# A layer trunk on one core: seven-product block multiplications in the feed-forwards, from four groups of k tiles to five, and their products redistributed over the stage

## The chip, the cores and the metric

One Trainium2 chip, one of its cores. The metric is the device time of one execution in microseconds (us); of several runs of a kernel the median is taken. A TensorE instruction works on tiles of 128 partitions; its results go to PSUM, whose banks hold 128x512 float32 each, and the kernel uses all eight of them. VectorE (DVE in the profile), ScalarE (ACT), GpSimd (POOL) and SyncE (SP) run beside TensorE (PE, and PEld for its weight loads), each in the order of its own instruction stream.

## What is computed

Two layers. Each is a half-step SwiGLU feed-forward, a token mixer, and a second half-step feed-forward, on 256 tokens of width 1024, so that four feed-forwards are run in all:

```python
def swiglu(x, w_in, w_out):
    gate, up = jnp.split(x @ w_in, 2, axis=-1)
    return (jax.nn.silu(gate) * up) @ w_out
...
for l in range(DEPTH):
    h = h + 0.5 * swiglu(rms_norm(h, ffn1_norm[l]), ffn1_w_in[l], ffn1_w_out[l])
    u = rms_norm(h, mix_norm[l])
    ...
    h = h + merged @ w_out[l]
    h = h + 0.5 * swiglu(rms_norm(h, ffn2_norm[l]), ffn2_w_in[l], ffn2_w_out[l])
return rms_norm(h, final_norm)
```

`w_in` is 1024 x 5632 and `w_out` 2816 x 1024, all float32. The change is about the second product of each feed-forward, (silu(gate) * up) @ w_out, whose contraction of 2816 is cut into 22 k tiles of 128. The mixer (a Mamba-2 branch and a gated DeltaNet branch) is not touched.

## The kernel before

**Precision by splitting.** Every float32 operand is split into a high part (rounded on ACT) and a low part (the rest, a subtraction on DVE). A product is three matmuls: high by high, high by low, low by high (`mm3` for token-stationary products at L335 to L337, `mm3w` for weight-stationary ones at L340 to L346). A weight tile of 128x1024 that has been split is called a form here: `prep` (L169 on) issues its ACT copy `whi` (L68) and its DVE subtraction `wlo` (L71).

**The weight stream.** `plan` lists the forms of the whole program in the order in which they are used, `stream` the loads. The loads go out on SP's queue into five buffers `wraw` (NRAW), the forms into five buffers each of `whi` and `wlo` (NSPL). `take` hands out the next form and on each call emits the preparation of forms up to four past it. After `state["hold"]` is set, it emits none beyond the form that it hands out. The tile framework allots a buffer of a pool when one is free, puts each engine's instructions in an order of its own making, by order of emission and by readiness in its model of time, and adds the waits.

**A feed-forward.** `ffn` runs the string `FFN`: `f` is the first 256 hidden columns with tokens stationary (four forms); each `c` is a chunk of 256 hidden channels' gate and up, 48 weight-stationary matmuls of 256 columns into one PSUM bank `fc` of the pool `accp` (four banks), with two forms. After a chunk ACT makes the SiLU (`sg`), DVE the product (`g`), and after every second chunk a pair of k tiles is split into the stationary operands `gh` and `gl`. Letters `A`, `B` and `d` are the second product, with tokens stationary, 128x512 at a time: token block t (two), column half n (two), k tile.

**Seven products for eight.** For the pairs of k tiles in `PAIRS` the 2x2x2 block product (two token blocks, two k tiles, two column halves) is done with seven products in the manner of Strassen and Winograd. Two pairs make a group. Each of a group's seven products is six 128x512 matmuls (two pairs by three) with one form; it would be eight directly. `block_sums` makes, per pair, four sums of 128x128 blocks on DVE and splits them (two ACT, two DVE instructions). The forms `q0` to `q2` have sums of weight tiles, each with one more DVE addition of 128x1024 in place; `q3` has a last addition done by an accumulating DMA on POOL's queue (`add_to`, L156), whose sum `q6` uses. The summed tile `wsum` stands in one of four buffers y0 to y3 from the first stage until its `q6`.

Before, the string is `f`, eight `c`, `A`, four `c`, `A`, four `c`, `A`, two `c`, `A`, two `c`, then `BdBBBddddd`. An `A` is four products of a group (into the four banks `p1`, `p5`, `p7`, `p6` of the pool `trp`), a `B` its other three, in the output banks `po` after the last chunk; two of a `B`'s forms are loaded a second time. Four groups cover 16 k tiles. The other six, `DIRECT`, are done directly by `d` (12 matmuls each).

**The end of a feed-forward.** `close_blocks` runs the `B`s and `d`s. `join` combines the four `p` banks into updates of the residual h, which go out as four accumulating DMAs on POOL's queue (L460). The last five `d` are taken at once and run token block 0 first: 30 matmuls, then 30 for token block 1. `residual` adds the `po` banks to h on DVE (`h<-o,h`); `norm_in` then makes the RMS norm of block 0, its eight PE transposes `hnT` being tied behind the sixth group of three matmuls of block 1 (`state["sums"][5]`), so that block 1's matmuls run during the norm. In the last feed-forward block 1's second column half is cut in two of 256 columns, the last of them in a bank `tail`.

Of the kernel before, what the change touches and what calls it, by code (L numbers as in the profile page):

```python
# [49 lines left out]
def trunk_kernel(ctx, tc, x, wst, wsm, norms, lpar, rpar, cst, out):  # L54
# [52 lines left out]
    def plan_ffn(j):  # L107


        o, j2, held = j + 4 * FC, j + 4 * FC + 22, []  # L110
# [63 lines left out]
    def prep(i):  # L174
        kind, js, _ = plan[i]
        hi = wpool.tile([P, 1024], F32R, tag="whi", name="whi", bufs=NSPL)
        lo = wpool.tile([P, 1024], F32R, tag="wlo", name="wlo", bufs=NSPL)
        r = raws[js[0]]
        with ExitStack() as behind:
            for ins in state["behind"].pop(i, ()):  # L180
                behind.enter_context(tc.issue_after(ins))
            state["whi"] = act(hi[:], r[:])
            if kind in ("q1", "q2"):
                to, by = (raws[k][:] for k in js[1:])
                tt(to, to, by, ALU.add)
# [7 lines left out]
        for k in {"q0": (), "q1": (), "q2": js[::2], "q3": ()}.get(kind, (js[0],)):  # L193
            raws.pop(k)
        halves[i] = (hi, lo)

# [247 lines left out]

    def block_products(todo, begin, end):

        for bank, st, prs in todo:
            wh, wl = take()
            for i, p in enumerate(prs):
                sh, sl = st(p)  # L450
                c = slice(i * 512, (i + 1) * 512)
                mm3(bank[:], sh, sl, wh[:, c], wl[:, c], begin and i == 0, end and i == 1)
# [21 lines left out]
    def close_blocks(po, stat, sums, pb, nw):  # L474

        direct, joined, n = list(DIRECT), join(pb), 0
        rest = FFN[FFN.rindex("c") + 1 :]
        for kind in rest[: len(rest) - NSPL]:  # L480
            if kind == "d":
                k = direct.pop(0)
                out_chunks(po, stat, [k], None, first=k == DIRECT[0])
                continue
            todo = [
                (po[0][1], lambda p: sums(p, 3), PAIRS[n]),
                (po[0][0], lambda p: stat(2 * p + 1, 0), PAIRS[n]),
                (po[1][0], lambda p: stat(2 * p + 1, 1), PAIRS[n]),
            ]
            block_products(todo, n == 0, False)  # L490
            n += 1
            if n % 2 == 0:
                next(joined)
        state["hold"] = True
        if nw is None:
            po.append(trb("tail"))
        out_chunks(po, stat, direct, direct[-1], group=NSPL, split=nw is None, first=False)
        return residual(po, nw)


    def ffn(nxt):
        gh = [slots.tile([P, 8, S], F32R, tag=t_, name="gh") for t_ in ("sA", "sB", "sC")]
# [1 line left out]

        bsa = slots.tile([P, 2, 2, 3, P], F32R, tag="sG", name="bsa")
        bsb = slots.tile([P, 16, P], F32R, tag="sH", name="bsb")
        bsc = slots.tile([P, 4, 2, P], F32R, tag="sI", name="bsc")
        bsd = s2.tile([P, 2, 2, P], F32R, tag="s2", name="bsd")
        bsb3 = bsb[:, 0:12].rearrange("p (i o j) t -> p i o j t", i=2, o=2)
        bsb1 = bsb[:, 12:16].rearrange("p (i o) t -> p i o t", i=2)  # L510

        def sums(p, j):

            q, i = (p - 1) // 2, (p - 1) % 2
# [3 lines left out]
            b = (bsc[:, 0:2], bsc[:, 2:4], bsb1, bsd[:])[q]  # L518
            return b[:, i, 0, :], b[:, i, 1, :]

        def block_sums(p, g2):

            sf = tmp2("sf")
            a11, a21, a12, a22 = (g2[:, j * P : (j + 1) * P] for j in range(4))
            s1, s2_, s3, s4 = (sf[:, j * P : (j + 1) * P] for j in range(4))
            tt(s1, a21, a22, ALU.subtract)
            tt(s3, a11, a21, ALU.subtract)
            tt(s2_, s1, a11, ALU.subtract)
            tt(s4, a12, s2_, ALU.add)
            q, i = (p - 1) // 2, (p - 1) % 2  # L530
# [20 lines left out]
        for t in range(2):  # L551
# [2 lines left out]
            tt(sg[:, 256:512], sg[:, 0:256], ps[t][:, 256:512], ALU.mult)  # L554
            gt.append(sg[:, 256:512])
        todo, pb, n, cut = FFN[1:], {}, 0, False
        for c in range(FC - 1):
            g2 = tmp2("g2")
            for a in range(2):
# [13 lines left out]
            split(2 * c + 2, g2[:].rearrange("p (k t) -> p k t", k=2))  # L573
            if c + 1 <= PAIRS[-1][-1]:
                block_sums(c + 1, g2)
            if todo[0] == "A":
                if not pb:
                    pb.update({i: trb(f"p{i}") for i in (1, 6, 5, 7)})
                four = [
                    (pb[1], lambda p: stat(2 * p, 0), PAIRS[n]),  # L580
                    (pb[5], lambda p: sums(p, 0), PAIRS[n]),
                    (pb[7], lambda p: sums(p, 2), PAIRS[n]),
                    (pb[6], lambda p: sums(p, 1), PAIRS[n]),
                ]
                block_products(four, n == 0, n == len(PAIRS) - 1)
                todo, cut = todo[1:], True
                n += 1
        po = [[accb("o"), accb("o")] for _ in range(2)]

        return close_blocks(po, stat, sums, pb, nxt)  # L590


    def mixer(l, nxt):
# [714 lines left out]
def _layout(inp):  # L1308
# [20 lines left out]
    def blocks(w):  # L1329
# [109 lines left out]
```

## Time and profile before

| | |
|---|---|
| time of three runs | 1543.58, 1544.32, 1544.55 us, median 1544.32 |
| span of the profiled execution, first to last instruction | 1539.7 us |
| PE, DVE, ACT, POOL busy | 99%, 80%, 61%, 5% of the span |
| mean rate of all DMA | 199 GB/s |
| feed-forwards in the trace (start to start of the next stage) | 591.7 to 769.2 us, 769.2 to 946.7 us, for instance |

The runs are 4.6 us longer than the profiled span at the median: what lies before the first and after the last instruction of the trace, and differences between executions. No other time of the profiled execution is given. A busy time counts from an instruction's start to its modelled end, and matmuls overlap one another, so that the step from one start to the next is what a matmul costs, not its duration; the same holds, by less, on DVE.

### The profile page before, as it was taken

To read this page: it belongs to the slowest core of one execution; us is meant where nothing else is said; L and a number is where in the kernel's file an instruction comes from. 1 tells how busy PE (TensorE), PEld (TensorE's weight loads), DVE (VectorE), ACT (ScalarE), POOL (GpSimd) and SP (SyncE) were. 2 spreads that over 40 slices of the span, in tenths; PEclk is the share of its full clock that TensorE was granted. 3 is DMA by queue.
4 is the path that set the end of the run, shared out by engine and by line. 5 is a ranking of instruction groups with operands and counts; after the bars stand their busy time and mean duration, and the time that the engine had idled before them with its cause. 6 is when DMAs were issued, how large, how long until landed. Compare 5 with 4: busy or idle time off the path is not lost.

```text
span 1539.7 us, 29072 instructions
## 1 busy us (share of the span) xinstructions
PE 1522.8 (99%) x11473; PEld 1384.4 (90%) x11473; DVE 1229.7 (80%) x1859; ACT 944.8 (61%) x1532; POOL 81.8 (5%) x92
## 2 busy tenths in 40 slices
PE   8999999999999999999999999999999999999998
PEld 7999889999888888999899998899998888899997
DVE  6878769967899766789778887689589996677886
ACT  5655667765665645555555566676756666455565
POOL 0000110000000000000100012010000000000010
PEclk9999999999999999999999999999999999999999
DMA  7687775653565556587867687665345555556785
GB/s 277 190 265 231 226 228 167 187 164 111 178 213 171 163 166 196 185 256 211 261 225 225 208 253 229 197 193 180 117 141 202 179 170 186 176 177 195 247 241 156
DMA packets 98831, 305.73 MB, mean 199 GB/s; under 512 B 22837, under 2 KB 23813, under 8 KB 97670
## 3 DMA queue, kind: packets, MB, share of 16 engines
q1 hardware_dynamic: 93796, 290.95, 57.2%
q0 software_dynamic: 4608, 12.58, 5.1%
q8 instruction: 90, 1.47, 0.4%
q14 instruction: 47, 0.39, 0.1%
q10 hardware_dynamic: 290, 0.33, 0.1%
HBM read 297.72 MB, written 1.92 MB: 195 GB/s over the span
## 4 chain that ended last, share of the span: by engine, by line
PE 89%; DVE 4%; ACT 2%; DMA 2%; issue 1%; SPq 1%; POOL 0%; POOLq 0%; ACTq 0%; DVEq 0%
PE fc L346 10%; PE fc L340 9%; PE fc L345 9%; PE t L366 9%; PE o L337 4%; PE o L335 4%; PE o L336 4%; PE f L366 3%; PE b L335 3%; PE b L337 3%; PE b L336 3%; PE p L336 2%; PE p L337 2%; PE p L335 2%; PE xs L345 1%; PE xs L340 1%
## 5 line engine op out<-in xcount | busy, mean ns | idle before, releaser
L71 DVE TENSOR_TENSOR wlo<-wraw,whi 128x1024 fp32r<-128x1024 f32 x488 | 591.8, 1221 | 186.7 <-ACT whi L68 172.2
L68 ACT ACTIVATE whi<-wraw 128x1024 fp32r<-128x1024 f32 x488 | 511.6, 1059 | 271.0 <-PE fc L345 92.5
L346 PE MATMUL fc<-uW,wlo 128*128 128x256 f32 x1280 | 354.9, 277 | 0.0
L340 PE MATMUL fc<-uW,whi 128*128 128x256 f32 x1280 | 354.1, 277 | 0.0
L345 PE MATMUL fc<-uW,whi 128*128 128x256 f32 x1260 | 348.3, 276 | 0.0
L340 PEld LDWEIGHTS fc<-uW,whi 128*128 128x128 f32 x1280 | 240.5, 188 | 0.8
L346 PEld LDWEIGHTS fc<-uW,wlo 128*128 128x128 f32 x1280 | 240.5, 188 | 0.0
L345 PEld LDWEIGHTS fc<-uW,whi 128*128 128x128 f32 x1260 | 236.5, 188 | 0.8
L366 PE MATMUL t<-whi,uW 128*128 128x512 f32 x512 | 165.3, 397 | 0.0
L366 PEld LDWEIGHTS t<-whi,uW 128*128 128x128 f32 x512 | 95.9, 188 | 21.6 <-issue 1.3
L68 ACT ACTIVATE whi<-wsum 128x1024 fp32r<-128x1024 f32 x64 | 68.0, 1062 | 58.8 <-PE fc L345 32.9
L366 PE MATMUL t<-wlo,uW 128*128 128x512 f32 x256 | 100.2, 392 | 0.0
L71 DVE TENSOR_TENSOR wlo<-wsum,whi 128x1024 fp32r<-128x1024 f32 x64 | 78.2, 1221 | 7.9 <-ACT whi L68 5.6
L335 PE MATMUL b<-whi,bh 128*128 128x512 f32 x192 | 76.1, 398 | 0.3
L336 PE MATMUL b<-wlo,bh 128*128 128x512 f32 x192 | 74.9, 390 | 0.0
L337 PE MATMUL b<-whi,bl 128*128 128x512 f32 x192 | 74.2, 393 | 0.0
L340 PE MATMUL xs<-uW,whi 128*128 128x256 f32 x256 | 72.8, 284 | 0.0
L346 PE MATMUL xs<-uW,wlo 128*128 128x256 f32 x256 | 71.4, 279 | 0.0
L345 PE MATMUL xs<-uW,whi 128*128 128x256 f32 x254 | 70.6, 278 | 0.0
L335 PE MATMUL o<-whi,gh 128*128 128x512 f32 (+1 forms) x160 | 62.0, 388 | 0.0
L337 PE MATMUL o<-whi,gl 128*128 128x512 f32 (+1 forms) x160 | 61.8, 386 | 0.0
L336 PE MATMUL o<-wlo,gh 128*128 128x512 f32 (+1 forms) x160 | 61.7, 386 | 0.0
(337 smaller groups left out, 3291.7 us busy)
## 6 DMA issues: line engine op xcount, KB each, us to landing
wraw<-in_wst_dram SPq DMA_DIRECT2D x504, 512.0 KB, 4.9
wsum<-in_wst_dram SPq DMA_DIRECT2D x16, 512.0 KB, 7.3
wsum<-in_wst_dram POOLq DMA_DIRECT2D x16, 512.0 KB, 8.7
dc<-rdram SPq DMA_DIRECT2D x8, 1024.0 KB, 8.5
nw<-in_norms_dram SPq DMA_DIRECT2D x6, 512.0 KB, 5.9
h<-u POOLq DMA_DIRECT2D x12, 256.0 KB, 6.8
gb<-rdram SPq DMA_DIRECT2D x8, 256.0 KB, 5.6
h<-in_x_dram SPq DMA_DIRECT2D x4, 256.0 KB, 3.7
```

The lines of the kernel that those rows point to most:

```text
L68: return A.activation(out=o, in_=i, func=func, **kw)
L71: return V.tensor_tensor(out=o, in0=a, in1=b, op=op)
L335: PE.matmul(ps, lh, rh, start=start, stop=False)
L336: PE.matmul(ps, lh, rl, start=False, stop=False)
L337: return PE.matmul(ps, ll, rh, start=False, stop=stop)
L340: PE.matmul(ps, wh, mh, start=start, stop=False)
L345: PE.matmul(ps, wh, ml, start=False, stop=False)
L346: PE.matmul(ps, wl, mh, start=False, stop=stop)
L366: ins = PE.matmul(ps[t][:], st, mv, start=k0 == 0 and j == 0, stop=k0 == KT - 2 and j == 5)
```

## The change

Five groups cover 20 of the 22 k tiles (`PAIRS` from (0, 1) to (8, 9)); two, 20 and 21, stay direct. An `A` is now five products: the three with plain sums as before, then the one with the block sum `sums(p, 3)` and the form `q4`, made from a tile that is loaded for the group anyway, into the output bank `po[0][0]`, then `q3`'s. `B` is one product with a form of its own; `E` is the product with `q6`, into `po[1][1]`. Two `E`s are done between chunks, ahead of the second and third `A`, three are kept for the end. A group's loads fall from six to five. `po[0][0]` and `po[1][1]` are taken from the pool `accp` while chunks still run. k tile 0 now has block sums too, for which its transposed bank is copied to `g0`. The column halves of the blocks and of `join`'s updates are exchanged. The end runs all five `B`s, then the two direct tiles for token block 0 (12 matmuls), then for block 1 the direct tiles' first half (6), three `E`s (18) and the direct tiles' second half (6).

```diff
-FFN = "f" + 8 * "c" + "A" + 4 * "c" + "A" + 4 * "c" + "A" + 2 * "c" + "A" + 2 * "c" + "BdBBBddddd"
-PAIRS = [(1, 2), (3, 4), (5, 6), (7, 8)]
-DIRECT = [0, 1, 18, 19, 20, 21]
+FFN = "f" + 5 * "c" + "A" + 4 * "c" + "EA" + 4 * "c" + "EA" + 4 * "c" + "A" + 2 * "c" + "A" + "c" + "BBBBB" + "ddEEE"
+PAIRS = [(0, 1), (2, 3), (4, 5), (6, 7), (8, 9)]
+DIRECT = [20, 21]
...
+                plan.append(("q4", (y + 2,), y + 3))
                 plan.append(("q3", (y, o + 3), y + 3))
-                held.append((y, o + 2))
+                held.append(y)
+                third.append(o + 3)
                 o += 4
+            elif kind == "E":
+                plan.append(("q6", (held.pop(0),), len(stream)))
             else:
-                y, b22 = held.pop(0)
-                stream.append(("w", b22))
-                plan.append(("q4", (len(stream) - 1,), len(stream)))
-                stream.append(("w", b22 + 1))
-                plan.append(("q5", (len(stream) - 1,), len(stream)))
-                plan.append(("q6", (y,), len(stream)))
+                plan_plain(third.pop(0), 1)
...
     def join(pb):
 
-        hv = [[h[:, t, n * 512 : (n + 1) * 512] for n in range(2)] for t in range(2)]
+        hv = [[h[:, t, n * 512 : (n + 1) * 512] for n in (1, 0)] for t in range(2)]
...
+    def fourth(q, po, stat, last=False):
+        return [(po[1][1], lambda p: stat(2 * p + 1, 1), PAIRS[q])], q == 0, last
+
+    def close_blocks(po, stat, pb, nw, kept):
+
+
+        joined, n = join(pb), 0
+        for q, two in enumerate(PAIRS):
+            block_products([(po[0][1], lambda p: stat(2 * p + 1, 0), two)], q == 0, False)
+            if q < 2:
                 next(joined)
         state["hold"] = True
         if nw is None:
             po.append(trb("tail"))
-        out_chunks(po, stat, direct, direct[-1], group=NSPL, split=nw is None, first=False)
+        ws = [take() for _ in DIRECT]
+        state["sums"] = []
+        for n in range(2):
+            direct(po[0][n][:], stat, 0, ws, slice(n * 512, (n + 1) * 512), False, True)
+        state["sums"] = []
+        direct(po[1][0][:], stat, 1, ws, slice(0, 512), True, True)
+        for q in kept:
+            state["sums"].extend(block_products(*fourth(q, po, stat)))
+        for c0, c1 in ((512, 1024),) if nw is not None else ((512, 768), (768, 1024)):
+            bank = po[2][:, 0:256] if c0 == 768 else po[1][1][:, 0 : c1 - c0]
+            direct(bank, stat, 1, ws, slice(c0, c1), c0 == 768, True)
         return residual(po, nw)
...
-        bsc = slots.tile([P, 4, 2, P], F32R, tag="sI", name="bsc")
-        bsd = s2.tile([P, 2, 2, P], F32R, tag="s2", name="bsd")
+        bsc = slots.tile([P, 2, 2, P], F32R, tag="sI", name="bsc")
...
+                    g0 = tmp2("g0")
+                    act(g0[:], bank[:])
                     split(0, bank[:].rearrange("p (k t) -> p k t", k=2))
+                    block_sums(0, g0)
...
+                if todo[0] == "E":
+                    if po[1][1] is None:
+                        po[1][1] = accb("o")
+                    block_products(*fourth(third[0], po, stat))
+                    third[0] += 1
+                    todo = todo[1:]
+                if todo[0] == "A":
+                    if not pb:
+                        pb.update({i: trb(f"p{i}") for i in (1, 6, 5, 7)})
+                        po[0][0] = accb("o")
+                    five = [
+                        (pb[1], lambda p: stat(2 * p, 0), PAIRS[n]),
+                        (pb[5], lambda p: sums(p, 0), PAIRS[n]),
+                        (pb[7], lambda p: sums(p, 2), PAIRS[n]),
+                        (po[0][0], lambda p: sums(p, 3), PAIRS[n]),
+                        (pb[6], lambda p: sums(p, 1), PAIRS[n]),
+                    ]
...
-                for r, c in ((0, 0), (0, 1), (1, 1), (1, 0)):
+                for r, c in ((0, 1), (0, 0), (1, 0), (1, 1)):
```

The block sums of two successive groups go to two sets of buffers in turn. The matmul order within a chunk after an `A` is as before: one 256-column matmul of it is done as two of 128 columns (`cut`, L342 and L343).

More of the change, by code (lines that the diff above doesn't have):

```diff
@@ L107, in plan_ffn @@
     def plan_ffn(j):
-        o, j2, held = j + 4 * FC, j + 4 * FC + 22, []
+        o, j2, held, third = j + 4 * FC, j + 4 * FC + 22, [], []
         for kind in FFN:
@@ L192, in prep @@
             add_to(r, js[1])
-        for k in {"q0": (), "q1": (), "q2": js[::2], "q3": ()}.get(kind, (js[0],)):
+        for k in {"q0": (), "q1": (), "q3": ()}.get(kind, (js[0],)):
             raws.pop(k)
@@ L451, in block_products @@
                 c = slice(i * 512, (i + 1) * 512)
-                mm3(bank[:], sh, sl, wh[:, c], wl[:, c], begin and i == 0, end and i == 1)
+                ins = mm3(bank[:], sh, sl, wh[:, c], wl[:, c], begin and i == 0, end and i == 1)
+                done.append(ins)
+        return done
     def join(pb):
-        hv = [[h[:, t, n * 512 : (n + 1) * 512] for n in range(2)] for t in range(2)]
+        hv = [[h[:, t, n * 512 : (n + 1) * 512] for n in (1, 0)] for t in range(2)]
         half, u2, u4, u3, u5 = (tmp2(n) for n in ("half", "u2", "u4", "u3", "u5"))
@@ L472, in join @@
         yield
[L474 to L492, printed above, removed]
+    def fourth(q, po, stat, last=False):
[5 more added lines that the diff above has]
+            if q < 2:
                 next(joined)
@@ L496, in close_blocks, with direct @@
             po.append(trb("tail"))
-        out_chunks(po, stat, direct, direct[-1], group=NSPL, split=nw is None, first=False)
-        return residual(po, nw)
+        ws = [take() for _ in DIRECT]
[9 more added lines that the diff above has]
+            direct(bank, stat, 1, ws, slice(c0, c1), c0 == 768, True)
+        return residual(po, nw)
+    def direct(bank, stat, t, ws, c, begin, end):
+        for i, (k, (wh, wl)) in enumerate(zip(DIRECT, ws)):
+            sh, sl = stat(k, t)
+            ins = mm3(bank, sh, sl, wh[:, c], wl[:, c], begin and i == 0, end and i == len(DIRECT) - 1)
+            state["sums"].append(ins)
     def ffn(nxt):
@@ L517, in sums @@
                 return b[:, i, 0, j, :], b[:, i, 1, j, :]
-            b = (bsc[:, 0:2], bsc[:, 2:4], bsb1, bsd[:])[q]
+            b = (bsc[:], bsb1)[q % 2]
             return b[:, i, 0, :], b[:, i, 1, :]
@@ L556, in ffn @@
         todo, pb, n, cut = FFN[1:], {}, 0, False
+        po, third = [[None, None], [None, None]], [0]
         for c in range(FC - 1):
@@ L571, in ffn @@
                             PE.transpose(bank[:, k * S + t * P : k * S + (t + 1) * P], gt[t][:, k * P : (k + 1) * P], ident)
+                    g0 = tmp2("g0")
+                    act(g0[:], bank[:])
                     split(0, bank[:].rearrange("p (k t) -> p k t", k=2))
[L573 to L587, printed above, removed]
@@ L588, in ffn @@
-        po = [[accb("o"), accb("o")] for _ in range(2)]
-        return close_blocks(po, stat, sums, pb, nxt)
+                    block_sums(0, g0)
+                if a == 1:
+                    split(2 * c + 2, g2[:].rearrange("p (k t) -> p k t", k=2))
+                    if c + 1 <= PAIRS[-1][-1]:
+                        block_sums(c + 1, g2)
+                if todo[0] == "E":
[4 more added lines that the diff above has]
+                    todo = todo[1:]
@@ new lines, in ffn @@
+                if todo[0] == "A":
[9 more added lines that the diff above has]
+                    ]
+                    for i, one_ in enumerate(five):
+                        block_products([one_], n == 0, n == len(PAIRS) - 1 and i != 3)
+                    todo, cut = todo[1:], True
+                    n += 1
@@ L593, in mixer @@
+        po[0][1], po[1][0] = accb("o"), accb("o")
+        return close_blocks(po, stat, pb, nxt, range(third[0], len(PAIRS)))
     def mixer(l, nxt):
```

5 lines of the change are left out of this document (3 added, 2 removed).

## The prediction

> **What bounds the kernel now.** First the page: its busy shares, the granted clock and the chain that ended last.
>
> ```profile
> span 1539.7 us, 29072 instructions
> PE 1522.8 (99%) x11473; PEld 1384.4 (90%) x11473; DVE 1229.7 (80%) x1859; ACT 944.8 (61%) x1532; POOL 81.8 (5%) x92
> PEclk9999999999999999999999999999999999999999
> PE 89%; DVE 4%; ACT 2%; DMA 2%; issue 1%; SPq 1%; POOL 0%; POOLq 0%; ACTq 0%; DVEq 0%
> ```
>
> PE is on the chain for 89% and its clock is never cut. A busy share can hide short stalls, so next the view of waits, for PE alone:
>
> ```profile
> PE hnT L282 <- DVE hn L74: 2.7, 2, 1.6
> PE nw L245 <- DMA row<-in_norms_dram: 2.3, 1, 2.3
> PE cbb L1045 <- DVE vb L71: 1.9, 2, 1.3
> PE xsb L1101 <- ACT xsT L68: 1.9, 2, 0.9
> PE wb L891 <- ACT Y L68: 0.8, 3, 0.3
> PE o L337 <- DVE ml L71: 0.6, 2, 0.3
> ```
>
> Columns: total us, times, longest. That is the whole list, 10.2 us, and none of it is a chunk or a product of a feed-forward: the start, the mixer, the seam after its output projection. Inside a feed-forward PE never waits, so there a matmul removed is worth its full step, as long as nothing else becomes late. How near that is, the windows view tells, for one feed-forward cut at products: four chunks and an A, again, two chunks and an A, two chunks, the end up to token block 0's last matmul, block 1:
>
> ```profile
> 828.85:856.22 27.37, 27.37 (x220) 26.42 (x218) 23.15 (x34) 16.28 (x22) 0.89 (x1) 1.00 0.72 230
> 856.22:883.58 27.36, 27.36 (x219) 26.41 (x218) 22.96 (x34) 16.27 (x22) 0.87 (x1) 1.00 0.73 233
> 883.58:900.07 16.49, 16.49 (x123) 15.54 (x122) 15.43 (x19) 9.91 (x13) 0.86 (x1) 1.00 0.80 254
> 900.07:916.56 16.49, 16.49 (x124) 15.54 (x122) 13.25 (x16) 10.13 (x13) 2.81 (x4) 1.00 0.91 279
> 916.56:942.30 25.74, 25.74 (x116) 21.32 (x115) 19.61 (x18) 16.37 (x18) 1.56 (x2) 1.00 0.90 264
> 942.30:950.30 8.00, 8.00 (x41) 6.70 (x40) 6.15 (x9) 5.45 (x8) 0.56 (x1) 1.00 0.32 108
> ```
>
> After the stretch come PE, PEld, DVE, ACT, POOL busy, clock, DMA share, GB/s. DVE is the next engine: 85% in a cycle of four chunks, 94% (15.43 of 16.49) in the third row, and PE still does not wait. ACT never exceeds 68%. In the end the DMA engines are 0.9 busy.
>
> **The matmuls removed.** A group's pair of k tiles costs 7 products where it cost 8, a product being 3 matmuls of 512 columns. Two more pairs in each feed-forward: 6 matmuls fewer, 24 in all. Their step, from PE's timeline (first and last of 18 in a row, then what follows):
>
> ```profile
> 942.41 0.39 PE L335 MATMUL o<-whi,gh 128*128 128x512 f32 x1
> ...
> 946.26 0.40 PE L337 MATMUL o<-whi,gl 128*128 128x512 f32 x1
> 946.50 1.04 PE L282 MATMUL hnT<-cs,hn 128*128 128x128 f32 x8
> ...
> 950.14 0.39 PE L366 MATMUL t<-whi,uW 128*128 128x512 f32 x1
> ```
>
> 3.85 us over 17 steps: 0.2265, with the group boundaries 0.227 us. So 24 x 0.227 = **5.45 us removed**. The Trainium skill's TensorE: Matmul & The Clock Gate, section Back-to-back issue gap, gives about 131 ns per matmul of 512 columns in a sustained stream; by that the gain would be 3.1 us. The row disagrees, and the row is these very instructions.
>
> **PE's small additions.** `cut` follows each A, now five times instead of four. Its cost, where 128-column matmuls stand for one of 256:
>
> ```profile
> 834.66 0.28 PE L340 MATMUL fc<-uW,whi 128*128 128x256 f32 x1
> 834.78 0.22 PE L342 MATMUL fc<-uW,whi 128*128 128x128 f32 x1
> 834.84 0.28 PE L343 MATMUL fc<-uW,whi 128*128 128x128 f32 x1
> 834.95 0.33 PE L346 MATMUL fc<-uW,wlo 128*128 128x256 f32 x1
> ```
>
> L342 to L346 is 0.17 us where one 256-column step is 0.12 (L340 to L342): 0.05 more, **+0.2 us** for four. In the last feed-forward 15 of the old matmuls ran as 30 halves, 6 of the new as 12; a half, 256 columns too, is put at 0.12, so that saves 0.1 us more.
>
> **Preparation.** Per feed-forward three more forms (35 + 2 against 28 + 6), three more weight additions (a fifth group) and two more pairs' block sums, one ACT copy (`g0`). The ACT group (columns: busy us, mean ns of one, idle before it), then DVE's timeline, to be read by its steps from start to start:
>
> ```profile
> L68 ACT ACTIVATE whi<-wraw 128x1024 fp32r<-128x1024 f32 x488 | 511.6, 1059 | 271.0 <-PE fc L345 92.5
> ```
>
> ```profile
> 826.43 0.55 DVE L71 TENSOR_TENSOR bsb<-sf,bsb 128x384 fp32r<-128x384 f32 x1
> 826.90 0.28 DVE L71 TENSOR_TENSOR bsc<-sf,bsc 128x128 fp32r<-128x128 f32 x1
> 827.10 0.41 DVE L71 TENSOR_TENSOR g<-sg,fc 128x256 f32<-128x256 f32 x1
> 827.43 1.21 DVE L71 TENSOR_TENSOR wlo<-wraw,whi 128x1024 fp32r<-128x1024 f32 x1
> 828.57 0.28 DVE L71 TENSOR_TENSOR sf<-g 128x128 f32<-128x128 f32 x1
> 828.77 1.21 DVE L71 TENSOR_TENSOR wlo<-wsum,whi 128x1024 fp32r<-128x1024 f32 x1
> ```
>
> `wlo` 1.14 (an addition of the same shape is taken equal), `g` 0.33, a block sum 0.2, the two splits 0.47 and 0.2: 1.5 us a pair. Added: 6 x 1.14 + 2 x 1.5 = 9.8 us of DVE and about 5 of ACT per feed-forward, beside shares of 80% and 61%. It is hidden in sum; what matters is the densest place. A chunk takes 5.5 us (of the fourth stretch's 16.49, 24 matmuls of the A are 5.45; half of the rest). The densest place is the new `EA`: from the end of the chunk before it (with its block sums) PE has one chunk and six products, 5.5 + 36 x 0.227 = 13.7 us. In that time DVE has three additions, the splits of `q1`, `q2`, `q4`, `q3` and of the next chunk's two forms, so 9 x 1.14 = 10.3, two `g`, one pair's block sums, and the split of the pair, taken at 0.6 from the 512-column share of a `wlo`: 10.3 + 0.7 + 1.5 + 0.6 = **13.1 us of 13.7, 96%**. The row with 94% and no PE wait is the nearest; five forms in hand are a reserve on top. I take 0, with bounds 0 and 0.5 us at each of 8 places. The fifth product alone does not thin DVE's reserve: an A of four asks 7 x 1.14 = 8.0 in 5.4 us, of five 8 x 1.14 = 9.1 in 6.8.
>
> **The banks.** After the first A three `accp` banks, after the first E two, are left to `fc`. A chunk's bank must then be free one chunk (5.5 us) after the chunk's end. `g` follows its chunk by one or two DVE operations of 1.14; taken at 0. Should it queue behind an A's preparation for longer, it adds to the stall of the EA places.
>
> **The loads.** One tile less per group, but 5 B and 2 direct tiles follow closely. Each tile is 0.52 MB. From the last A's start to block 0's end there are now 21.8 us (5 x 6 + 5 x 6 + 12 matmuls of 0.227, and a chunk) with 12 loads, one accumulate among them, and four updates of h: some 7.3 MB, 335 GB/s, where the rows above have 279 and 264 with the queues 0.9 busy. But the loads are issued up to ten forms ahead, so I take 0, with 0 to 1 us for each feed-forward.
>
> **The seams.** Token block 1 still covers block 0's norm with 30 matmuls, and the transposes are still tied to the eighteenth. Rows of DVE:
>
> ```profile
> 942.61 0.69 DVE L74 SCALAR_TENSOR_TENSOR h<-o,h 128x512 f32<-128x512 f32 x1 [2.71 <-PE o L337]
> 944.10 0.21 DVE L79 TENSOR_SCALAR zz<-ss 128x1 f32<-128x1 f32 x1 [0.79 <-ACT junk L68]
> 945.05 1.42 DVE L74 SCALAR_TENSOR_TENSOR hn<-h,zz,nw 128x512 f32<-128x512 f32 x2 [0.74 <-POOL zz L210]
> 946.39 1.22 DVE L71 TENSOR_TENSOR wlo<-wraw,whi 128x1024 fp32r<-128x1024 f32 x1
> ```
>
> The first half of `hn` is ready at 945.75, its transposes start at 946.50: 0.7 us in hand. New in front of this chain is the last E's split, emitted within the end (1.14 us, ready about when block 0 ends). And the next stage's first form needs a buffer: before, the first of five direct tiles was free after 6 of the 30 matmuls; now both direct tiles are needed to the end, and the first buffer to fall free is the first E's, after 12, 1.4 us later. With 1.06 for `whi` and 1.14 for `wlo` it is ready some 2.5 us before the seam, where it was ready earlier. I take 0.2 us a seam, three seams: **+0.6**, bounds 0 and 2 us each.
>
> `join` has 0.23 x 42 = 9.6 us from the first B to block 0's end where it had 26. Its landing time, from the view of that line:
>
> ```profile
> DMA to landing us min/median/max: 4.5/6.4/10.0
> ```
>
> The `p` banks are complete a chunk before the first B, so that the updates can be issued around the first B's start; block 0's are the first two and fit. With the halves exchanged the last update goes to block 1's half that is finished first, 6 matmuls after block 0, 11 us from the first B, against a longest landing of 10.0. Taken at 0; bounds within the seams'.
>
> **The tail.** Before, 15 matmuls of 256 columns, 1.80 us, lay between block 1's last two pieces; now 6, 0.72 us:
>
> ```profile
> 1531.64 0.69 DVE L74 SCALAR_TENSOR_TENSOR h<-o,h 128x512 f32<-128x512 f32 x1 [0.38 <-PE o L337]
> 1533.44 0.42 DVE L74 SCALAR_TENSOR_TENSOR h<-tail,h 128x256 f32<-128x256 f32 x1 [0.37 <-PE tail L337]
> 1533.90 0.42 DVE L71 TENSOR_TENSOR fo<-h,nw 128x256 f32<-128x256 f32 x1
> 1534.44 0.21 DVE L79 TENSOR_SCALAR zz<-ssf 128x1 f32<-128x1 f32 x1
> ```
>
> The first piece's addition will end about when the second's can start; its product with the norm's weight (0.46 as a step, 1533.44 to 1533.90) then falls behind the last matmul: **+0.5 us**, bounds 0 and 0.6.
>
> **The sum**, on the profiled span: -5.45 + 0.2 - 0.1 + 0.6 + 0.5 = -4.25, so 1539.7 becomes 1535.4. The median stands 4.6 us above the span and I carry it over: 1544.3 - 4.2 = **1540.1 us**.
>
> **The rivals.** (1) DVE becomes the bound in EA. Additions, ACT copies and subtractions of `q0` to `q3` wait for each other in turn (q1's copy needs q0's addition), and the 0.6 us spare there is little. From 0.6 us of such gaps on, and the lead of the forms in hand used up, PE waits. A wait of one addition, 1.14 us, at 8 places is 9.1 us: 1540.1 + 9.1 = 1549.2, slower. For it speaks the 96%; against it the 94% row and that PE has waited for no form so far. The Trainium skill, VectorE: DVE Perf Modes, section The DRAIN you can't avoid, says that the next operation starts only when the pipe is empty; at the duration of 1.21 instead of the step of 1.14, nine operations take 0.6 us more and the places would be full. The rows show the next start 0.07 before the recorded end, so this trace does not bear it out. Chance 0.14.
> (2) The seam: if the first form's buffer came from the direct tiles, in turn, instead of from the first free one, it could be prepared only at the end: ACT's copy, DVE's 1.14 and the handoffs, less the 0.7 us of its other tile's last matmuls, about 2 us at three seams, 6 less the 0.6 counted: 1545.5, within 0.2% of before. Against it: banks of one pool are already held across others. Chance 0.1.
> (3) Loads or h's updates come late in the shorter end: 0.5 to 1 us in each of four, 1542 to 1544, no change. The DMA shares of 0.9 speak for it, the depth of the queue against. Chance 0.15.
> (4) A removed matmul is worth less than its step, since something beside PE sets part of the pace; at the step of 256 columns, 0.12, all 24 save 2.9 us: 1542.7. PE without waits speaks against it. Chance 0.02. The Trainium skill's 131 ns (page and section above) would come to about the same.
> The forecast itself: 0.59, its own range 1538.7 to 1541.2.
>
> **The numbers.** About 0.2%, 3.1 us, is what a measurement of this kernel can tell from no change: faster is below 1541.2, slower above 1547.4. Faster: the forecast's 0.59. Same: (2), (3), (4), and a little of (1), 0.28. Slower: most of (1), 0.13. The range goes from the full saving with nothing lost, 1538.6, up to 1546.0, which takes in (2), (3) and the milder part of (1).
>
> **What would show it.** Right: the windows of a feed-forward are 1.0 to 1.4 us shorter each, PE's list of waits gains nothing at `p`, `o` or `fc`, and DVE is 95% busy ahead of the second and third A. Rival 1 shows as PE or PEld waiting for `wlo` at `p` lines or at a chunk's start; rival 2 as a wait for `whi` at the first `f` or `t` matmul; rival 3 as ACT `whi` waiting for `wraw`, or `h<-o,h` for a DMA. Wrong outright: spans of the feed-forwards unchanged or longer with PE never waiting, which would mean that the step of the other matmuls has changed.

## The result and the profile after

The changed kernel takes 1560.35 us (median of four, 1558.73 to 1561.22), the kernel before in the same session 1543.95 (1542.68 to 1544.55): a ratio of 1.0108, interval 1.0093 to 1.0122. It is 16 us slower, where 4 us faster was forecast. The profiled span went from 1539.7 to 1558.0.

The page of the kernel after, its head and its chain:

```profile
span 1558.0 us, 29073 instructions
PE 1528.9 (98%) x11444; PEld 1381.5 (89%) x11444; DVE 1267.6 (81%) x1931; ACT 958.8 (62%) x1564; POOL 86.1 (6%) x96
...
PE 65%; DVE 15%; DMA 9%; ACT 5%; issue 5%; SPq 1%; POOL 0%; POOLq 0%; ACTq 0%; DVEq 0%
```

The mean granted clock is 0.999, as before. PE's share of the chain fell from 89% to 65%, and DVE, DMA and ACT took its place. The view of PE's waits, in the columns of the prediction (total, times, longest), shows where:

```profile
PE hnT L281 <- DVE hn L74: 5.6, 5, 1.8
PE o L335 <- DVE wlo L71: 3.0, 4, 0.8
...
PE fc L339 <- DVE g L71: 2.2, 4, 1.0
PE p L336 <- DVE bsa L71: 1.6, 3, 0.6
...
PE p L336 <- DVE gl L71: 0.3, 1, 0.3
```

All five stand in or at the end of feed-forwards; before, there were only the two waits for `hn`. This view counts only time in which PE has nothing left in its pipe. Measured instead by how late PE's starts are against their step, all four feed-forwards together lose about 4.8 us between matmuls of chunks (`fc`), 3.9 at the last A (`p`), 5.5 in the end (`o`) and 3.2 at the three seams (`hnT`). Before, the second feed-forward lost nothing by this measure. It runs here from its first matmul at 601.95 to the next one's at 783.55, 181.6 us, and ran from 595.16 to 772.64, 177.5. All four feed-forwards together are 14.6 us longer than before in the profiles, and the two mixers 2.9.

What lies behind one chunk wait shows the chain followed back from it, in order of time (start, duration, what). The stretch is that of the first E and the A after it, and the two chunks behind them:

```profile
676.65 2.37 DVE wlo L71 x2
679.01 0.02 issue
679.03 9.10 DMA wraw<-in_wst_dram
...
688.23 1.07 ACT whi L68
...
689.33 1.23 DVE wlo L71
690.55 0.34 DVE g L71
...
690.94 0.39 PE fc L339
```

A split on DVE frees a raw buffer, and 0.02 us later the load that waited for it is issued. It lands 9.1 us after that. ACT's copy `whi` of this tile stands ahead of the chunk's `sg` in ACT's queue, so `g`, whose chunk had ended by 684.5, comes at 690.5. With only two banks left to `fc`, PE waits for it. ACT's timeline shows the order:

```profile
681.67 1.06 ACT L68 ACTIVATE whi<-wraw 128x1024 fp32r<-128x1024 f32 x1 [2.76 <-DMA wraw<-in_wst_dram]
686.29 1.06 ACT L68 ACTIVATE whi<-wraw 128x1024 fp32r<-128x1024 f32 x1 [3.56 <-DMA wraw<-in_wst_dram]
688.23 1.06 ACT L68 ACTIVATE whi<-wraw 128x1024 fp32r<-128x1024 f32 x1 [0.88 <-DMA wraw<-in_wst_dram]
689.20 0.36 ACT L68 ACTIVATE sg<-fc 128x256 f32<-128x256 f32 x1
```

In the whole kernel these waits of ACT for raw tiles are 77.5 us, where they were 29.1. The windows of the same place show why the loads are late (after the stretch: PE, PEld, DVE, ACT, POOL busy, clock, DMA share, GB/s):

```profile
657.00:664.81 7.81, 7.81 (x72) 7.81 (x70) 6.06 (x12) 4.41 (x7) 0.00 (x0) 1.00 0.83 308
664.81:678.76 13.95, 13.95 (x89) 12.54 (x88) 13.74 (x18) 10.19 (x14) 0.87 (x1) 1.00 0.23 68
678.76:684.30 5.54, 5.54 (x50) 5.54 (x49) 3.94 (x5) 1.21 (x2) 0.00 (x0) 1.00 0.94 216
684.30:690.94 6.64, 5.66 (x51) 5.46 (x50) 2.80 (x4) 2.42 (x4) 0.00 (x0) 1.00 1.00 379
```

The second row is the densest place of the prediction: DVE 13.74 of 13.95 us busy (forecast 13.1 of 13.7), and PE does not wait in it. But the DMA queues are nearly idle there, 68 GB/s: all five raw buffers stand full until DVE comes to the splits that free them. Then the loads are issued one behind the other as the splits go by, the queues fill (0.94, then 1.00 at 379 GB/s), and in the last row PE loses 1 us.

The end of a feed-forward has the same pattern. The second direct tile's load is issued when a B's split frees its buffer, and lands 10.2 us later, beside three of the four updates of h on GpSimd's queue (issued 762.44 to 763.76; the first had landed at 759.37). The chain there:

```profile
758.59 1.23 DVE wlo L71
759.82 0.02 issue
759.84 10.20 DMA wraw<-in_wst_dram
...
770.14 1.07 ACT whi L68
...
771.24 1.24 DVE wlo L71
...
772.52 0.50 PE o L335
```

PE starts this matmul 1.03 us late. The same wait stands in each of the four feed-forwards.

### The profile page after: what moved, and what is told of

The parts are those of the page before. It is cut to its first block, busy times and chain, and to the rows that moved or that the text cites. A ratio compares the mean times of both kernels' runs of the same rounds, so it can differ in the third digit from the quotient of the medians.

```text
span 1558.0 us, 29073 instructions
## 1 busy us (share of the span) xinstructions
PE 1528.9 (98%) x11444; PEld 1381.5 (89%) x11444; DVE 1267.6 (81%) x1931; ACT 958.8 (62%) x1564; POOL 86.1 (6%) x96
## 4 chain that ended last, share of the span: by engine, by line
PE 65%; DVE 15%; DMA 9%; ACT 5%; issue 5%; SPq 1%; POOL 0%; POOLq 0%; ACTq 0%; DVEq 0%
PE t L365 9%; DMA wraw<-in_wst_dram 7%; DVE wlo L71 7%; PE fc L339 5%; PE fc L345 5%; PE fc L344 5%; PE f L365 3%; PE b L336 3%; PE b L334 3%; PE b L335 3%; ACT whi L68 2%; PE o L336 2%; PE o L335 2%; PE o L334 2%; PE xs L339 1%
## 5 line engine op out<-in xcount | busy, mean ns | idle before, releaser
L71 DVE TENSOR_TENSOR wlo<-wraw,whi 128x1024 fp32r<-128x1024 f32 x484 | 583.2, 1221 | 176.3 <-ACT whi L68 166.1
L68 ACT ACTIVATE whi<-wraw 128x1024 fp32r<-128x1024 f32 x484 | 506.2, 1058 | 265.6 <-DMA wraw<-in_wst_dram 77.5
L68 ACT ACTIVATE whi<-wsum 128x1024 fp32r<-128x1024 f32 x80 | 83.5, 1053 | 56.5 <-DVE wsum L71 28.1
L71 DVE TENSOR_TENSOR wlo<-wsum,whi 128x1024 fp32r<-128x1024 f32 x80 | 96.9, 1220 | 7.9 <-ACT whi L68 7.0
L365 PEld LDWEIGHTS t<-wlo,uW 128*128 128x128 f32 x256 | 48.2, 188 | 10.2 <-DVE wlo L71 0.2
L68 ACT ACTIVATE gh<-g 128x512 fp32r<-128x512 f32 x40 | 25.3, 633 | 44.3 <-DVE g L71 44.2
L71 DVE TENSOR_TENSOR wsum<-wsum,wraw 128x1024 f32<-128x1024 f32 x40 | 48.8, 1221 | 0.5
```

Source lines behind the costliest of these rows:

```text
L68: return A.activation(out=o, in_=i, func=func, **kw)
L71: return V.tensor_tensor(out=o, in0=a, in1=b, op=op)
L365: ins = PE.matmul(ps[t][:], st, mv, start=k0 == 0 and j == 0, stop=k0 == KT - 2 and j == 5)
```

## The experiments

Theory L: the raw tiles are loaded late for want of buffers, and everything queued behind ACT's waiting copies is late with them. Rival D: VectorE is full, and the late loads are only its consequence. Two smaller ones concern the end: the updates of h (C), and the order of the seam's work (S). Each group of runs has its own runs of the kernel before beside it, 1543.0 to 1543.6 us; ratios are to those.

**A sixth raw buffer.** The groups can spare one of their four first-tile buffers, since the early E's free theirs; it takes every sixth raw tile of a feed-forward.

```
-        m, room = need, NRAW
...
-            room -= stream[m][0] == "w"
+            room -= stream[m][0] == "w" and m not in sixth
...
-            state["first"] = (state["first"] + 1) % 4
+            state["first"] = (state["first"] + 1) % 3
+        elif j in sixth:
+            r = slots.tile([P, 1024], F32, tag="y3", name="wraw")
...
+        inner = [i for i in range(s0, len(stream)) if stream[i][0] == "w"]
+        sixth.update(inner[NRAW::6])
```

> The changed kernel with a sixth buffer for raw weight tiles inside the feed-forwards (one of the four first-tile buffers of the groups, which it can spare), nothing else. Theory L (raw tiles are issued late because all five raw buffers stand full while the forms wait their turn; ACT then stands at a copy whose tile has not landed, and everything queued behind it is late: g and so the chunk's bank, the block sums, the direct tiles, hn at the seam): ACT's 77.5 us of waiting for raw tiles falls to below 35, the PE waits at chunk starts (4.8 us in all four feed-forwards), at the last A (3.9) and at the end (5.5 and 3.2 at the seams) fall to less than half, and the time to 1548 to 1553, at best some 1543. Rival D (VectorE is full in the stretch of an E and an A, and the late loads are only its consequence): less than 3 us gained, 1557 or more, with the chunk and A waits as they are. Rival S (the end's own order): the 8.7 us of the end and the seams stay, and the rest shrinks: 1553 to 1556.

Measured: 1541.88 us, ratio 0.999 (0.998 to 1.0), 18 us less than the changed kernel and more than theory L allowed at best. PE's list of waits has no chunk, no product and no direct tile of a feed-forward any more (`o<-ml` is the mixer):

```profile
PE hnT L286 <- DVE hn L74: 5.2, 4, 2.4
PE cbb L1070 <- DVE vb L71: 2.5, 2, 1.8
PE nw L249 <- DMA row<-in_norms_dram: 2.2, 1, 2.2
...
PE o L341 <- DVE ml L71: 0.6, 2, 0.3
```

The waits at the seams went down to 0.86, 0 and 0.45 us. ACT's waits for raw tiles fell to 28.0 us. Theory S is out, but for the seam. The windows of this kernel at the same matmuls as the last three rows above:

```profile
660.56:674.51 13.95, 13.95 (x89) 12.54 (x88) 13.74 (x18) 10.35 (x14) 0.87 (x1) 1.00 0.24 60
674.51:680.05 5.54, 5.54 (x50) 5.53 (x49) 3.98 (x6) 2.13 (x2) 0.00 (x0) 1.00 0.92 220
680.05:685.70 5.65, 5.65 (x52) 5.65 (x52) 3.25 (x6) 1.98 (x4) 0.00 (x0) 1.00 1.03 415
```

VectorE is as full as in the changed kernel, the queues are as quiet and then as full, and the first load after the pause goes out as long ahead of the stretch's end, 4.6 us (669.96 here, 674.20 in the changed kernel). But it is the 219th weight load on SP's queue where it was the 218th: one more tile is in hand, and PE does not wait. So with six buffers the full stretch on VectorE costs PE nothing, and neither do the busy queues behind it.

**The silu ahead of the waiting copies.** The last two forms that are prepared during the chunk after an A come behind that chunk's `sg`.

```
+                if cut:
+                    state["cap"] = state["prepped"]
                 chan_chunk(ps, cut or (c, a) == (1, 0))
...
-                act(sg[:], ps[:, 0:S], AF.Silu)
+                first = act(sg[:], ps[:, 0:S], AF.Silu)
...
+                if cut:
+                    for i in range(2):
+                        state["behind"][state["cap"] + i] = [first.ins]
+                    state["cap"], cut = n_forms, False
```

> The changed kernel, but the two forms that are prepared during the chunk after an A come behind that chunk's silu on ACT instead of ahead of it; no load and no operation is added or taken away. Theory L with ACT's queue as the link: the waits of PE for g at chunk starts (4.8 us in four feed-forwards) go, the waits at the end and the seams (8.7) stay; the last A's 3.9 may halve, since its block sums come from chunks too: 1552 to 1556. Rival D: the silu was late because DVE and ACT are full, the order does not matter: within 2 us of 1560.

Measured: 1559.88 us, ratio 1.0109 (1.0092 to 1.0126): nothing gained. The waits for `g` are gone, as theory L had it, but the held-back forms are now late themselves:

```profile
PE p L334 <- ACT whi L68: 6.0, 8, 1.0
PE o L335 <- DVE wlo L71: 3.6, 7, 0.6
```

The time is rival D's and the reason is neither's. ACT waits only 30.0 us for raw tiles here, but with the held-back copies behind the silu it now waits for the ends of chunks, 3.4 us in the changed kernel:

```profile
ACT sg L68 <- PE fc L345: 108.4, 28, 5.9
```

Ahead of the last A of the second feed-forward, all tiles asked for so far had landed by 750.72, and ACT copies the next two from 752.19 on. The chain there goes back over DVE to `sg` and the chunk's end at 745.6, with no load in it. So there the order itself makes the forms late, not the loads; in the end of the feed-forward the direct tiles still land late. The run does not separate theory L from rival D.

**The early E's spread.**

```
-FFN = "f" + 5 * "c" + "A" + 4 * "c" + "EA" + 4 * "c" + "EA" + 4 * "c" + "A" + ...
+FFN = "f" + 5 * "c" + "A" + 4 * "c" + "A" + 2 * "c" + "E" + 2 * "c" + "A" + 2 * "c" + "E" + 2 * "c" + "A" + ...
```

> The changed kernel with its two early E's two chunks ahead of the third and the fourth A instead of directly ahead of the second and the third. No place has six forms in a row any more, and until the first E there are three banks for the chunks. Rival D (VectorE at 96% in the stretch of an E and an A): the waits at chunk starts and at the A's go, 5 to 9 us gained, 1551 to 1555. Theory L: an E needs no load of its own, so the raw tiles come as late as before: waits at chunk starts shrink only where a third bank is free, 1 to 3 us gained, 1557 to 1559; ACT's waiting for raw tiles stays above 60 us.

Measured: 1553.34 us, ratio 1.0072 (1.0057 to 1.0087), 5.6 us gained by the ratios and 7 by the medians, in rival D's range. No wait at an A or for a bank is left, and ACT's waits for raw tiles fall to 33.4 us, which theory L had expected to stay above 60. The end is no better: its waits for splits are 3.0 us as before, and two for copies, 0.5 us in sum, are new. So how dense the stretch is does count with five buffers; that it counts through the time at which buffers come free is argued here; the run with less work for VectorE below bears on it.

**Without the updates of h.**

```
         def onto(o, u):
-            G.dma_start(out=o, in_=u[:], accum_op=ALU.add)
+            pass
```

> The changed kernel without the four additions of the block products to h by GpSimd's DMA at the end of each feed-forward (that part of h's update is left out). They land in 7 to 11 us beside the last direct tile, which lands 10.2 us after its issue. If their traffic makes the direct tiles late (theory C): the PE wait of 1.0 us at the direct tiles and the 1.1 us at the seams go, 7 to 9 us gained, 1551 to 1553, and the chunk and A waits stay. Theory L (the direct tiles are issued late, for want of a raw buffer, whatever else moves): the issue times stay and only the landing shortens: 2 to 4 us gained, 1556 to 1558.

Measured: 1553.79 us, ratio 1.0076 (1.0058 to 1.0093), 5 us gained by the ratios and 6.5 by the medians, between the two ranges or at the lower end of theory C's. The loads of that place are issued at the same times in both kernels. The view of their line over the same stretch, first the changed kernel, then this one:

```profile
L170 SPq DMA_DIRECT2D wraw<-in_wst_dram x3: 328/328/328, 758.7 to 761.6; - x3
DMA to landing us min/median/max: 8.8/10.2/11.1
```

```profile
L170 SPq DMA_DIRECT2D wraw<-in_wst_dram x3: 328/328/328, 758.7 to 761.6; - x3
DMA to landing us min/median/max: 6.9/7.2/7.4
```

3.0 us of the 10.2 are the updates' traffic, and without it PE waits for no direct tile. The chunk and A waits stay. Either one more tile in hand (the sixth buffer) or a quicker landing cures the end.

**Less work for VectorE, five buffers.**

```
-                    if c + 1 <= PAIRS[-1][-1]:
+                    if c + 1 <= PAIRS[1][-1]:
                         block_sums(c + 1, g2)
```

> The changed kernel, five raw buffers as it has, without the block sums of the pairs from the fifth k tile pair on (their seven operations on VectorE and two on ACT are left out, the products read the sums of earlier pairs). In the stretch of an E and an A VectorE was busy 13.74 of 13.95 us; 1.5 us or more of that goes. Rival D, now in its strongest form (VectorE's full stretch delays the splits that free the raw buffers, and so causes the late loads): 6 us or more gained, 1554 or less, ACT's waiting for raw tiles well below 50 us. Theory L alone (the buffers stand full because PE takes only two forms per chunk ahead of the stretch, and five are too few to load in that time what is asked after it, however fast VectorE is): 0 to 3 us gained, 1557 to 1560, ACT's waiting still above 60 us; the last A's waits for block sums (3.9 us) may go with the sums themselves.

Measured: 1547.28 us, ratio 1.0031 (1.0012 to 1.0049), 12 us gained by the ratios and 13 by the medians, as rival D had it. ACT still waits 76.3 us for raw tiles, as theory L had it. Its windows of the same place, each cut at the same matmuls:

```profile
660.70:674.60 13.90, 13.90 (x89) 12.52 (x88) 13.67 (x14) 9.97 (x12) 0.87 (x1) 1.00 0.26 76
674.60:690.00 15.40, 15.40 (x137) 15.36 (x137) 8.70 (x10) 6.36 (x9) 0.00 (x0) 1.00 0.97 329
```

DVE is still full in the stretch (13.67 of 13.90) and the DMA queues still idle and then full, but the first load after the pause goes out 5.7 us ahead of the stretch's end (668.88), where it went out 4.6 us ahead (674.20 against 678.76). The shift is 1.2 us, about the size of the longest chunk wait, 1.14 us, and in the last row PE no longer waits. So both theories hold a part: five buffers stand full through the quiet time, and VectorE's pace sets when the burst of loads can begin; one more buffer or an earlier burst is enough. The waits at the seams are still there, and those for the direct tiles in part (1.6 us in PE's list, where it was 3.0). Block sums that come earlier help the last A besides; how the 12 us divide between the two is not separated.

**The kernel before with four raw buffers.** `NRAW = 5` becomes `NRAW = 4`.

> The kernel before with four raw buffers instead of five; nothing else. Theory L as a general law of these feed-forwards (the number of raw buffers bounds how early the loads are issued, and five was just enough for the old order): the same pattern appears there, ACT waiting for raw tiles for over 70 us (29 before) and PE waits at chunks, products and direct tiles, 10 to 40 us slower, 1553 to 1583; in the mixers too. Rival: the old order had loads to spare, under 4 us slower.

Measured: 1574.74 us, ratio 1.0204 (1.0171 to 1.0236), 31 us slower, from two executions only (1570.48 and 1579.01). The buffer is missing in the mixers too: in the profiled execution, the slower one, 28.0 of 37.5 us are the feed-forwards' and 9.5 the mixers'. ACT waits 107.2 us for raw tiles, and PE for splits and copies in the end; waits at chunks, which theory L had expected, did not come:

```profile
PE o L336 <- DVE wlo L71: 9.8, 15, 0.8
PE o L335 <- ACT whi L68: 3.4, 6, 1.4
```

The old order had not a buffer to spare. That could not be seen in its list of PE's waits, which had none inside a feed-forward.

**The first term by itself.** The kernel before, one product of the second group left out in each feed-forward, its form prepared.

```
-                block_products(four, n == 0, n == len(PAIRS) - 1)
+                block_products(four[:3], n == 0, n == len(PAIRS) - 1)
+                if n == 1:
+                    take()
+                else:
+                    block_products(four[3:], n == 0, n == len(PAIRS) - 1)
```

> The kernel before with one product of the second group (6 matmuls of 512 columns) left out in each feed-forward, its weight form prepared all the same; this part of the sum is left out of the output. It measures the first term by itself: 24 matmuls at 0.227 us are 5.45 us, 1537.5 or so, 0.9965. If a removed matmul is worth only 0.12 to 0.13 us (rival 4 of the prediction): 1540.0. If the forms' preparation comes late at once where PE is 1.36 us faster: no gain, 1542 to 1543.

Measured: 1538.09 us, ratio 0.9965 (0.9955 to 0.9975), 5.4 us for 24 matmuls.

**The seam.** Six buffers, and block 0's additions to h emitted ahead of the last E's split.

```
...
+        if nw is not None:
+            with tc.high_priority(offset=PRI):
+                for n in range(2):
+                    hv = h[:, 0, n * 512 : (n + 1) * 512]
+                    state["early"] = stt(hv, po[0][n][:], 0.5, hv, ALU.mult, ALU.add)
+            state["late"][state["taken"] + len(kept) - 1] = state["early"]
```

> Six raw buffers as in the run before, and at the seam the last E's split on VectorE behind block 0's additions to h instead of ahead of them. With six buffers PE waited for hn for 0.86, 0 and 0.45 us at the three seams; VectorE did three splits of E's, 3.5 us in a row, before the first addition. If that order is the seam's price (theory S for the seam): these waits fall below 0.1, 1 to 1.5 us gained on the six buffers alone, 1540.5 or so. If the seam waits for something else (the second bank, the rsqrt on GpSimd): no more than 0.3 gained and hn as late as before.

Measured: 1540.11 us, ratio 0.9979 (0.997 to 0.9988), 0.2% faster than the kernel before. The waits are below 0.1, 0.37 and 0; all three were expected below 0.1. DVE's timeline of the second seam, first the changed kernel, then this one:

```profile
772.38 3.49 DVE L71 TENSOR_TENSOR wlo<-wsum,whi 128x1024 fp32r<-128x1024 f32 x3
775.78 1.88 DVE L74 SCALAR_TENSOR_TENSOR h<-o,h 128x512 f32<-128x512 f32 x3
```

```profile
761.82 2.35 DVE L71 TENSOR_TENSOR wlo<-wsum,whi 128x1024 fp32r<-128x1024 f32 x2
764.09 0.68 DVE L74 SCALAR_TENSOR_TENSOR h<-o,h 128x512 f32<-128x512 f32 x1
765.21 0.69 DVE L74 SCALAR_TENSOR_TENSOR h<-o,h 128x512 f32<-128x512 f32 x1 [0.44 <-PE o L341]
765.82 1.21 DVE L71 TENSOR_TENSOR wlo<-wsum,whi 128x1024 fp32r<-128x1024 f32 x1
...
768.06 0.69 DVE L74 SCALAR_TENSOR_TENSOR h<-o,h 128x512 f32<-128x512 f32 x1 [0.90 <-DMA h<-u]
768.66 1.40 DVE L74 SCALAR_TENSOR_TENSOR hn<-h,zz,nw 128x512 f32<-128x512 f32 x2
```

In the changed kernel three splits, all queued behind the late direct tile, stand ahead of the additions. Here DVE waits for PE instead. What is left, 0.37 us, is an addition of block 1 that stands ahead of `hn` and waits for an update of h on its way.

**Both repairs and the spreading.** The kernel of the seam run with the E's spread as above.

> The same, with the two early E's spread as in the third run. Theory L: with six buffers no wait was left at the chunks and A's, so spreading gives nothing more: within 1 us of the run beside it, 1540 to 1541.5. Rival D: VectorE's full stretch still costs something that the waits do not show (mixer, later work): 2 us or more below the run beside it.

Measured: 1543.33 us, ratio 1.0003 (0.9994 to 1.0013), 3.2 us slower than the run without the spreading, which neither theory had. PE has no wait for it; its matmuls are slower. 96 matmuls of 256 columns, two chunks after an E, from 685.28 to 696.58:

```profile
685.28 0.28 PE L344 MATMUL fc<-uW,whi 128*128 128x256 f32 x1
...
696.58 0.39 PE L339 MATMUL p<-whi,gh 128*128 128x512 f32 x1
```

11.30 us, 0.1177 a matmul, where other chunks have 0.1135. Only the chunk after an A had its `cut`. The last run gives it to the chunk after an E as well:

```
                     third[0] += 1
-                    todo = todo[1:]
+                    todo, cut = todo[1:], True
```

> The run with six buffers, spread E's and the seam's order, with the first chunk after an E cut as the first chunk after an A is. In that run the two chunks after each spread E took 5.65 us each where the others take 5.44 to 5.48, 0.4 us per E, 8 E's, 3.2 us, and it was 3.2 us slower than the same kernel without the spreading. If the missing cut is the reason: all chunks at 5.48 and 5.44 again, 3 us gained, 1540 to 1540.5, like the kernel without the spreading. If the spreading costs by something else: as before, 1543.

Measured: 1541.17 us, ratio 0.9984 (0.9975 to 0.9994). The same two chunks take 11.03 us (the last row is the product after them, the cut adds one instruction):

```profile
684.05 0.28 PE L344 MATMUL fc<-uW,whi 128*128 128x256 f32 x1
...
695.08 0.39 PE L339 MATMUL p<-whi,gh 128*128 128x512 f32 x1
```

The missing cut cost 0.27 us a place by these rows, 2.2 us at eight, which is the difference of the two medians (by the ratios it is 2.9). It was also missing in the run with the spread E's and five buffers, whose gain from the spreading alone should be larger by as much. With six buffers and the cut in place, spreading gives nothing: 0.8 us more than the run without it, within the intervals.

## Why the prediction was wrong

**The step that failed** is the one on the loads: "the loads are issued up to ten forms ahead, so I take 0, with 0 to 1 us for each feed-forward". Five of these ten are prepared forms; a load can be issued only when one of five raw buffers is free, and a buffer is free only when DVE is done with its tile. The step compared 335 GB/s with 279 and 264 as means. In the trace the queues ran at 68 GB/s while the buffers stood full, then at 379 with the tiles landing 9 to 11 us after their issue. With six buffers the queues run in the same way, and no tile is late for PE: what was missing is one tile in hand when the pause begins. One more buffer took back 18 us; one fewer in the old kernel, its mixers included, cost 31.

**Preparation and banks, taken at 0.** DVE's load was sized well, and PE indeed waits for no form in that stretch. What the step left out is the second thing a split does, to free a buffer. The bank step said that "`g` follows its chunk by one or two DVE operations"; it came some 6 us after its chunk, behind ACT copies whose tiles had not landed. The condition was named ("should it queue behind an A's preparation"), but not that a load could be what it queues behind.

**The seams, +0.2 each**, were 1.06 to 1.10. The last E's split was counted as one operation, ready about when block 0 ends. All three kept E's were split in that place, 3.5 us in a row, behind the late direct tile. With six buffers they are still in a row, but earlier against PE: 0.44 was left on average, and with the order changed 0.1. The seam's first form did not wait for a buffer, so rival 2 has no part.

**The tail, +0.5**, was less: the first piece's product did fall behind the last matmul, but from that matmul's start to that of `zz` it is 1.48 us (1550.87 to 1552.35) where it was 1.32 (1533.12 to 1534.44). From `zz` to the end of the trace the changed kernel took another 0.35 us more, which the kernel of the seam run did not (5.26 us there, 5.27 before); that the two together make 0.5 is luck.

**The matmuls, -5.45**, were right: 5.4 by the direct test, 0.225 us each; rival 4 is out. The 131 ns of the Trainium skill (TensorE: Matmul & The Clock Gate, section Back-to-back issue gap) would make an estimate of 3.1 us, which this run does not bear out.

**The rivals.** Rival 3 had the cause and its sign, ACT's `whi` waiting for `wraw`, but only in the end and at 0.5 to 1 us each; the end and its seams were 8.7 us, and the same cause worked in the middle too. Rival 1 put the slow side on DVE's full stretch; its symptoms came, its mechanism only by a detour: PE was late not in the stretch but two chunks after it, because with five buffers VectorE's pace delays the loads. The sum of PE's terms holds where the loads are not late: with both repairs the four feed-forwards are 1.11, 0.55, 1.19 and (with the tail) 1.19 us shorter than before in the profiles, 4.0 together, against a forecast of 4.25 for them. The agreement of that kernel's 1540.11 with the forecast time is partly chance, since the profiled mixers, which no edit touches, were 2.3 and 0.5 us longer in it. In all profiles with five groups the mixers are longer than before, by 0.1 to 2.5 us, and in the old kernel with 24 matmuls fewer by 0.2 to 0.3. Whether that is the change or the spread of executions is left open, as is whether a sixth buffer would help the old order, for which there is no room.

## What to carry to other kernels

An empty list of PE's waits says nothing about how many load buffers are to spare, and the DMA share by windows does not either: with five buffers and with six the same quiet stretch stands ahead of the same full one. Adding a buffer here, and taking one from the old kernel, told it. Count how far ahead a load can be issued in buffers, by what frees each of them and how late that operation can be, not in prepared forms. Where an in-order engine both prepares later work and clears earlier results, each can hold up the other: here a late tile held up the silu, and with the silu put ahead the forms were held up, for the same time in all.

## What the runs showed that was not expected

A run of 256-column matmuls behind a group of 512-column ones went at a step of 0.1177 us through 96 matmuls, 0.1135 where one matmul of the first chunk is cut into two of 128 columns. The DMA queues carried 379 GB/s at a share of 1.00 in the window above, and 415 with six buffers. A 512 KB tile landed 8.8 to 11.1 us after its issue beside others and the updates of h, 6.9 to 7.4 without those updates, and 5.0 in the median over the kernel after.
